# Transposing the B and C projections by DMA instead of on TensorE in a one-core hybrid SSD and attention layer

## The chip, the cores and the metric

The kernel runs on one core of a Trainium2 chip. The metric is the device time of one execution in microseconds (us), as the median of several runs. Engine names: PE is TensorE (PEld its weight loads), DVE is VectorE, ACT is ScalarE, POOL is GpSimd and SP is SyncE, which here issues the loads.

## The reference

One decoder layer on 256 tokens of width 2048, all in float32. What matters here is the state-space (SSD) group at its start:

```python
proj = rmsnorm(h) @ w_in                                  # z | x,B,C | dt | q | k | v
xbc = silu(causal_dwconv(xbc, conv_w, conv_b))            # 4 taps along the tokens, one filter a channel
xs, bm, cm = split(xbc)                                   # x: 2048 channels, B and C: 4 groups x 128 each
dt = softplus(dt_raw + dt_bias)
cb = einsum('bclgn,bcsgn->bgcls', Cc, Bc)                 # per group and chunk of 128 tokens
y_diag = einsum('bgecls,bcsgep->bclgep', cb * decay_in, X)
states = einsum('bclgn,bgecl,bclgep->bcgepn', Bc, decay_states, X)
```

After it come the gate z, a grouped norm, sliding-window attention, the output projection, a feed-forward part with a convolution of 3 taps, and a gated embedding.

## The kernel before

**Products.** Each product of 256 tokens goes in chunks of 512 columns. A weight slab (256 rows by 512 columns) is loaded on SP's queue (line 207, tile `w`, 7 slots), rounded to a short float on ACT (line 192, `wh`, 4 slots), its rest is taken on DVE (line 193, `wl`, 4 slots), and PE makes three products of each (lines 219 to 221, or 317 to 319 for B and C). So a slab of one chunk is 12 matmuls (2 row blocks, 2 token blocks, 3 products) and a chunk of the input projection is 8 slabs. A chunk's sums stand in a pair of PSUM tiles, `acc0` and `acc1`, one for each 128 tokens, in two buffers.

**Order.** B and C are computed together over all 16 row blocks while `xT` is loaded, and fill both pairs of `acc`; the products for dt come behind them (lines 337, 338). Then the code treats B, then C (lines 387 to 390), then the chain of dt (lines 392 to 435: transposed dt at line 394, softplus, running sums, a copy `scr` in DRAM), then group by group x, z, the scan and the gate (`ssd_x`, `ssd_gate`, `ssd_end`). The compiler's planner orders each engine's instructions by a simulated timeline, so they stand in its queue in another order than in the code; an engine then works strictly in the order of its queue and waits at its head.

**B and C.** `evac_scaled` (line 348) copies each half of the sums to SBUF on ACT (line 352, tiles `ct0`, `ct1`, one buffer, which C shares with B). `conv_chunk` (line 272) transposes it on PE, 4 channel blocks by 2 token blocks, so 8 transposes for B and 8 for C (line 279), into `tr`, a PSUM tile with two buffers. `conv_tile` (line 263) then makes the first tap on ACT (line 266) and three taps on DVE (line 268) out of PSUM into `BT` or `CT`. A SiLU on ACT follows (line 390). The `tr` tiles are taken in code order, so the one for dt (line 392) comes after the four of B and C. `BT` is read by the transpose at line 465 and with `CT` by the matmuls at line 456; `CT` again at line 499. x goes through the same `conv_chunk` (line 471).

**The feed-forward part** (lines 825 to 844) has the same convolution done in another way: ACT copies the sums to `u` (line 831), POOL takes the 32-bit numbers apart into two halves of 16 bits (line 833, `half`), SP issues a transposing DMA (line 835, `flip`), POOL puts the halves together (line 836, `uc`), and the convolution reads `uc` in SBUF (line 843).

Of the kernel before, what the change touches and what calls it, by code (L numbers as in the profile page):

```python
# [14 lines left out]
U16 = mybir.dt.uint16  # L15
# [5 lines left out]
P = 128  # L21
T = 256
NB = T // P
# [3 lines left out]
NC = 512  # L27
# [38 lines left out]
def hybrid_layer(  # L66
# [20 lines left out]
    nc = tc.nc  # L87
    V, S, G, PE = nc.vector, nc.scalar, nc.gpsimd, nc.tensor
# [13 lines left out]
    def nm(s):  # L102
        uid[0] += 1
        return f"{s}_{uid[0]}"
# [3 lines left out]
    def sb(pool, shape, tag, dt=F32, bufs=None):  # L108
        kw = {} if bufs is None else {"bufs": bufs}
        size = math.prod(shape[1:]) * (2 if dt in (mybir.dt.bfloat16, U16) else 4)  # L110
        tags = sizes.setdefault(pool.id, {})
        tags[tag] = max(tags.get(tag, 0), -(-size // 32) * 32 * (bufs or pool.bufs))
        return pool.tile(shape, dt, tag=tag, name=nm(tag), **kw)
# [7 lines left out]
    def acc_pair():  # L121
        return [ps_acc.tile([P, NC], F32, tag=f"acc{b}", name=nm(f"acc{b}")) for b in range(NB)]

    def tr_tile():
        return ps_tr.tile([P, NC], F32, tag="tr", name=nm("tr"))
# [14 lines left out]
    def load_first(k, pieces=1):  # L140

        xt = sb(xin, [P, T], "xt", bufs=6)
        nc.sync.dma_start(xt, xT[:, k, :])
        w = sb(wp, [P, KW, NC], "w", bufs=WR)
        n = KW // pieces
        for c in range(0, KW, n):
            cs = slice(c, c + n)
            nc.sync.dma_start(w[:, cs, :], w_in[cs, k // KW, :, (k % KW) * NC : (k % KW + 1) * NC].rearrange("c p n -> p c n"))
        return w, xt
# [26 lines left out]
    scw = sb(const, [P, 24 * 5], "scw")  # L176
# [86 lines left out]
    def conv_tile(ps, dst, taps, bias):  # L263

        n = len(taps)
        S.activation(out=dst, in_=ps, func=AF.Identity, scale=taps[n - 1], bias=bias)
        for s in range(1, n):
            V.scalar_tensor_tensor(  # L268
                out=dst[:, s:], in0=ps[:, : T - s], scalar=taps[n - 1 - s], in1=dst[:, s:], op0=ALU.mult, op1=ALU.add
            )  # L270

    def conv_chunk(src, dst, cw, ntap, c0):

        for half in range(2):
            tr = tr_tile().rearrange("p (a t) -> p a t", a=2)
            for i in range(2):
                f = half * 2 + i
                for b in range(NB):
                    PE.transpose(tr[:, i, b * P : (b + 1) * P], src[b][:, f * P : (f + 1) * P], ident)
            for i in range(2):  # L280
                f = half * 2 + i
                w = cw[:, (c0 + f) * (ntap + 1) : (c0 + f + 1) * (ntap + 1)]
                conv_tile(tr[:, i, :], dst[:, f, :], [w[:, j : j + 1] for j in range(ntap)], w[:, ntap : ntap + 1])
# [13 lines left out]
    acc_b, acc_c = acc_pair(), acc_pair()  # L297
    with xin_:
        wd = sb(xin, [P, KT, 32], "wd")
        dhl = sb(xin, [P, KT, 64], "dhl", F32R)  # L300
        for k in range(KT):
            w, xt = first[k] if k < len(first) else load_first(k)
# [23 lines left out]
            if k in (5, 9):  # L326
                b = k // 4 - 1
# [20 lines left out]
    def evac_scaled(acc, pool, tag, bufs=None):  # L348
        res = []
        for b in range(NB):  # L350
            t = sb(pool, [P, NC], f"{tag}{b}", bufs=bufs)
            S.activation(out=t, in_=acc[b], func=AF.Copy, scale=rx[:, b : b + 1])
            res.append(t)
        return res
# [29 lines left out]
    with tc.tile_pool(name="ssd", bufs=1) as sp, tc.tile_pool(name="dram", bufs=1, space=bass.MemoryType.DRAM) as dp:  # L384
        BT = sb(sp, [P, 4, T], "BT")
        CT = sb(sp, [P, 4, T], "CT")
        for c, (acc, dst) in enumerate(((acc_b, BT), (acc_c, CT))):
            t = evac_scaled(acc, sp, "ct", 1)
            conv_chunk(t, dst, scw, 4, 16 + 4 * c)
            S.activation(out=dst, in_=dst, func=AF.Silu)  # L390

        tr = tr_tile()
# [137 lines left out]
        with tc.tile_pool(name="rope", bufs=1) as rp:  # L530
# [3 lines left out]
            for j in range(HALF):  # L534
                f = float(np.float32(THETA) ** np.float32(-2.0 * j / ROPE))
# [332 lines left out]
    with tc.tile_pool(name="ple", bufs=2) as lp:  # L868
# [5 lines left out]
        for n in range(4):  # L874
            acc = acc_pair()
# [77 lines left out]
```

## Time and profile before

| | |
|---|---|
| median of 3 runs | 1437.21 us (1435.33 to 1437.77) |
| the profiled execution | 1435.81 us, of which its span from the first to the last instruction is 1434.1 us |
| busy share of the span | PE 99%, PEld 81%, DVE 69%, ACT 55%, POOL 20% |
| granted clock of PE | 0.999 of full speed |
| DMA | 292.62 MB, 204 GB/s on average |

Times in the rows are counted from the start of the span. The duration of a matmul overlaps the next one's, so what a matmul costs is read from the distance of two starts. An entry "[1.09 <-ACT ct L352]" says that the engine stood idle for 1.09 us before and that ACT's instruction of line 352 ended this. B and C are summed up until about 54 us, and the first reading of `CT` is at 105 us.

### The profile page before, as it was taken

The numbers are of one execution on the slowest core, as the hardware profiler recorded it, in microseconds if no ns is written. First come the engines' busy times: TensorE is split into PE (matmuls) and PEld (weight loads), VectorE is DVE, ScalarE is ACT, GpSimd is POOL, SyncE is SP. The second block draws the span as 40 slices with busy tenths as digits, with TensorE's granted clock in tenths as the row PEclk, the third lists the DMA queues.
The fourth block names the chain that finished last, engine by engine and source line by source line (L and its number), as shares of the span: only waits on it lengthen the run. The fifth ranks groups of instructions, "written<-read, shape, count | busy, mean of one in ns | idle before, by whom it ended". The sixth has DMA issues, their size and how long they took to land.

```text
span 1434.1 us, 18053 instructions
## 1 busy us (share of the span) xinstructions
PE 1421.9 (99%) x6516; PEld 1166.2 (81%) x6516; DVE 995.0 (69%) x1240; ACT 792.0 (55%) x1067; POOL 288.2 (20%) x234
## 2 busy tenths in 40 slices
PE   9999999999999999999999999999999999999998
PEld 6887888888877777888888888888888888888886
DVE  6678876766789889656667646765675577476854
ACT  6575555544576655556556446545554554455643
POOL 0002010008535422013143103201320131120000
PEclk9999999999999999999999999999999999999999
DMA  9666656556787777577787777867876876776671
GB/s 338 217 190 202 201 177 189 163 160 205 191 236 198 213 203 223 171 208 209 217 231 198 217 196 216 228 194 202 226 208 194 221 214 205 206 207 190 209 223 66
DMA packets 163466, 292.62 MB, mean 204 GB/s; under 512 B 93040, under 2 KB 95920, under 8 KB 162992
## 3 DMA queue, kind: packets, MB, share of 16 engines
q1 hardware_dynamic: 162944, 290.99, 69.8%
q8 instruction: 51, 0.84, 0.2%
q10 hardware_dynamic: 432, 0.48, 0.1%
q14 instruction: 39, 0.32, 0.1%
HBM read 268.32 MB, written 2.13 MB: 189 GB/s over the span
## 4 chain that ended last, share of the span: by engine, by line
PE 61%; DVE 1%; issue 0%; ACT 0%; DVEq 0%
PE acc L220 20%; PE acc L221 20%; PE acc L219 20%; PE tr L252 0%; DVE wl L193 0%; PE tr L731 0%; DVE h L359 0%; DVE den L713 0%; DVE sg L883 0%; ACT s L709 0%; DVE yl L193 0%; DVE s L698 0%; DVE nm L705 0%; DVE sg L884 0%; ACT sg L882 0%
## 5 line engine op out<-in xcount | busy, mean ns | idle before, releaser
L193 DVE TENSOR_TENSOR wl<-w,wh 128x1024 fp32r<-128x1024 f32 (+1 forms) x493 | 637.8, 1298 | 370.9 <-ACT wh L192 370.1
L192 ACT CAST wh<-w 128x1024 fp32r<-128x1024 f32 (+1 forms) x493 | 514.8, 1049 | 496.6 <-PE acc L221 446.5
L220 PE MATMUL acc<-wl,ah 128*128 128x512 f32 x1280 | 499.8, 390 | 1.2 <-DVE wl L193 1.2
L221 PE MATMUL acc<-wh,al 128*128 128x512 f32 x1280 | 499.7, 391 | 0.0
L219 PE MATMUL acc<-wh,ah 128*128 128x512 f32 x1280 | 498.6, 391 | 0.0
L220 PEld LDWEIGHTS acc<-wl,ah 128*128 128x128 f32 x1280 | 240.4, 188 | 51.6 <-DVE wl L193 1.6
L219 PEld LDWEIGHTS acc<-wh,ah 128*128 128x128 f32 x1280 | 240.4, 188 | 50.8 <-issue 1.2
L221 PEld LDWEIGHTS acc<-wh,al 128*128 128x128 f32 x1280 | 240.4, 188 | 50.1 <-issue 0.5
L221 PE MATMUL acc<-wh,gl 128*128 128x512 f32 x352 | 137.0, 389 | 0.0
L220 PE MATMUL acc<-wl,gh 128*128 128x512 f32 x352 | 137.0, 389 | 0.0
L219 PE MATMUL acc<-wh,gh 128*128 128x512 f32 x352 | 136.4, 389 | 0.0
L833 POOL COPY half<-u 128x1024 uint16<-128x1024 uint16 x44 | 60.7, 1393 | 263.1 <-ACT u L831 263.1
L219 PE MATMUL acc<-wh,yh 128*128 128x512 f32 x256 | 101.3, 396 | 0.8 <-DVE h L359 0.8
L220 PE MATMUL acc<-wl,yh 128*128 128x512 f32 x256 | 100.0, 391 | 0.6 <-DVE wl L193 0.6
L221 PE MATMUL acc<-wh,yl 128*128 128x512 f32 x256 | 99.6, 390 | 0.0
L836 POOL COPY uc<-flip 128x1024 uint16<-128x1024 uint16 x44 | 55.7, 1265 | 166.3 <-DMA flip<-half 166.3
L220 PEld LDWEIGHTS acc<-wl,gh 128*128 128x128 f32 x352 | 66.1, 188 | 13.7
L221 PEld LDWEIGHTS acc<-wh,gl 128*128 128x128 f32 x352 | 66.1, 188 | 13.7
L219 PEld LDWEIGHTS acc<-wh,gh 128*128 128x128 f32 x352 | 66.1, 188 | 13.6
L359 DVE TENSOR_TENSOR h<-h,acc 128x512 f32<-128x512 f32 x112 | 72.6, 677 | 1.1 <-PE acc L221 1.1
L268 DVE SCALAR_TENSOR_TENSOR cv<-uc,fcw,cv 128x254 f32<-128x254 f32 (+1 forms) x176 | 73.0, 475 | 0.0
L219 PEld LDWEIGHTS acc<-wh,yh 128*128 128x128 f32 x256 | 48.0, 188 | 14.4 <-issue 4.3
(229 smaller groups left out, 1129.5 us busy)
## 6 DMA issues: line engine op xcount, KB each, us to landing
w<-in_w_up_dram SPq DMA_DIRECT2D x176, 512.0 KB, 3.9
w<-in_w_in_dram SPq DMA_DIRECT2D x126, 512.0 KB, 4.1
w<-in_w_down_dram SPq DMA_DIRECT2D x88, 512.0 KB, 4.2
w<-in_w_out_dram SPq DMA_DIRECT2D x64, 512.0 KB, 4.2
w<-in_w_pg_dram SPq DMA_DIRECT2D x32, 512.0 KB, 4.3
seg<-scr SPq DMA_DIRECT2D x8, 512.0 KB, 5.4
xt<-in_xT_dram SPq DMA_DIRECT2D x16, 128.0 KB, 6.5
h<-in_x_dram SPq DMA_DIRECT2D x2, 1024.0 KB, 8.6
```

Of the source, the lines that this page charges most:

```text
L192: S.copy(hi, src)
L193: V.tensor_tensor(out=lo, in0=src, in1=hi.bitcast(F32), op=ALU.subtract)
L219: PE.matmul(acc[b], lhsT=hi, rhs=wh[:, i, :], start=(k == 0), stop=False)
L220: PE.matmul(acc[b], lhsT=hi, rhs=wl[:, i, :], start=False, stop=False)
L221: PE.matmul(acc[b], lhsT=lo, rhs=wh[:, i, :], start=False, stop=(k == total - 1))
L268: V.scalar_tensor_tensor(out=dst[:, s:], in0=ps[:, : T - s], scalar=taps[n - 1 - s], in1=dst[:, s:], op0=ALU.mult, op1=ALU.add)
L359: V.tensor_tensor(out=hs, in0=hs, in1=acc[b], op=ALU.add)
L833: G.tensor_copy(half.rearrange("p (a n) -> p a n", a=2), u_.bitcast(U16).rearrange("p (n a) -> p a n", a=2))
L836: G.tensor_copy(uc[:, :, b * P : (b + 1) * P].bitcast(U16).rearrange("p f (t a) -> p f t a", a=2), flip.rearrange("p (a f) t -> p f t a", ...
```

## The change

B and C are no longer transposed on PE. ACT evacuates B's sums to `ct` as before and C's to tiles of their own (`yc0`, `yc1`). For each half of 128 tokens, POOL takes the numbers apart into 16-bit halves, SP issues a transposing DMA and POOL puts the halves together in a tile `raw`; the convolution reads `raw` in SBUF. B uses the slots of tiles that come later (`z`, `Xd`, `xc`), C uses new ones (`xh`, `xf`, `xt`). The convolution's own instructions stay as they are, and x keeps its transposes on PE.

```diff
-        for c, (acc, dst) in enumerate(((acc_b, BT), (acc_c, CT))):
-            t = evac_scaled(acc, sp, "ct", 1)
-            conv_chunk(t, dst, scw, 4, 16 + 4 * c)
+        for c, (acc, dst, tags) in enumerate(((acc_b, BT, ("ct", "z", "Xd", "xc")), (acc_c, CT, ("yc", "xh", "xf", "xt")))):
+            t = evac_scaled(acc, sp, tags[0], 1 + c)
+            raw = sb(sp, [P, 4, T], tags[3])
+            for b in range(NB):
+                half = sb(sp, [P, 2 * NC], f"{tags[1]}{b}", U16)
+                G.tensor_copy(half.rearrange("p (a n) -> p a n", a=2), t[b].bitcast(U16).rearrange("p (n a) -> p a n", a=2))
+                flip = sb(sp, [P, 8, P], f"{tags[2]}{b}", U16)
+                nc.sync.dma_start_transpose(flip, half)
+                G.tensor_copy(
+                    raw[:, :, b * P : (b + 1) * P].bitcast(U16).rearrange("p f (t a) -> p f t a", a=2),
+                    flip.rearrange("p (a f) t -> p f t a", a=2),
+                )
+            for f in range(4):
+                i = 16 + 4 * c + f
+                w = scw[:, i * 5 : (i + 1) * 5]
+                conv_tile(raw[:, f, :], dst[:, f, :], [w[:, j : j + 1] for j in range(4)], w[:, 4:5])
             S.activation(out=dst, in_=dst, func=AF.Silu)
```

## Rows read from the trace of the kernel before

**Rows 1.** The page, busy time of an engine: us (share of the span) and instructions.
```profile
PE 1421.9 (99%) x6516; PEld 1166.2 (81%) x6516; DVE 995.0 (69%) x1240; ACT 792.0 (55%) x1067; POOL 288.2 (20%) x234
```

**Rows 2.** PE's waits over the whole span: us in total, times, longest us.
```profile
PE acc L220 <- DVE wl L193: 1.8, 2, 1.2
PE tr L279 <- ACT ct L352: 1.1, 1, 1.1
```

**Rows 3.** Timeline of PE, 56 to 125 us: start us, us, what.
```profile
56.74 0.41 PE L279 MATMUL tr<-ident,ct 128*128 128x128 f32 x2 [1.09 <-ACT ct L352]
56.90 0.48 PE L219 MATMUL acc<-wh,ah 128*128 128x512 f32 x1
...
60.17 0.39 PE L221 MATMUL acc<-wh,al 128*128 128x512 f32 x1
...
61.31 0.39 PE L220 MATMUL acc<-wl,ah 128*128 128x512 f32 x1
61.54 0.82 PE L279 MATMUL tr<-ident,ct 128*128 128x128 f32 x6
62.11 0.48 PE L219 MATMUL acc<-wh,ah 128*128 128x512 f32 x1
62.42 0.40 PE L220 MATMUL acc<-wl,ah 128*128 128x512 f32 x1
...
86.80 0.63 PE L394 MATMUL tr<-sel,hsq 64*128 64x32 f32 x4
...
104.99 0.60 PE L456 MATMUL ms<-CT,BT 128*128 128x128 f32 x4
...
124.21 0.50 PE L220 MATMUL acc<-wl,ah 128*128 128x512 f32 x1 [1.15 <-DVE wl L193]
```

**Rows 4.** Lines 833, 836 and 835: duration ns min/median/max, first and last start.
```profile
L833 POOL COPY half<-u x44: 1037/1043/2039, 630.5 to 1263.1; 128x1024 uint16<-128x1024 uint16 x44
L836 POOL COPY uc<-flip x44: 1155/1164/2112, 639.0 to 1273.5; 128x1024 uint16<-128x1024 uint16 x44
L835 SPq DMA_TRANSPOSE flip<-half x44: 1237/1239/1590, 634.4 to 1267.6; - x44
DMA to landing us min/median/max: 3.7/5.4/6.6
```

**Rows 5.** Timeline of ACT, one chunk of the feed-forward part: evacuation and convolution.
```profile
629.77 0.69 ACT L831 ACTIVATE u<-acc,rh 128x512 f32<-128x512 f32 x1 [0.37 <-PE acc L221]
...
645.63 2.08 ACT L266 ACTIVATE cv<-uc,fcw 128x256 f32<-128x256 f32 x4
```

**Rows 6.** Who waited for line 836 over the whole span: us, times.
```profile
  ACT cv L266: 4.7, 5
```

**Rows 7.** Timeline of POOL, 33 to 112 us: its first work after 33 us.
```profile
111.03 1.88 POOL L448 TENSOR_SCALAR_AFFINE_SELECT seg<-seg 128x1024 f32<-128x1024 f32 x1 [77.70 <-ACT wh L192]
```

**Rows 8.** Waits of SP's queue, 0 to 320 us: us in total, times, longest us.
```profile
SPq L207 <- DVE wl L193: 207.4, 84, 9.0
```

**Rows 9.** Groups of DVE, 45 to 110 us: busy us, mean ns, idle before.
```profile
L193 DVE TENSOR_TENSOR wl<-w,wh 128x1024 fp32r<-128x1024 f32 x20 | 24.4, 1221 | 12.1 <-ACT wh L192 11.7 <-issue 0.2
L268 DVE SCALAR_TENSOR_TENSOR BT<-tr,scw,BT 128x254 f32<-128x254 f32 x4 | 1.9, 475 | 0.0
```

**Rows 10.** The same groups, 630 to 1275 us, the feed-forward part.
```profile
L193 DVE TENSOR_TENSOR wl<-w,wh 128x1024 fp32r<-128x1024 f32 x238 | 312.4, 1315 | 235.9 <-ACT wh L192 235.9
L268 DVE SCALAR_TENSOR_TENSOR cv<-uc,fcw,cv 128x254 f32<-128x254 f32 x84 | 38.6, 475 | 0.0
```

**Rows 11.** Timeline of ACT, 62 to 65 us: the first tap of B and the next cast.
```profile
62.06 0.57 ACT L266 ACTIVATE BT<-tr,scw 128x256 f32<-128x256 f32 x1 [3.31 <-PE tr L279]
...
64.12 1.06 ACT L192 CAST wh<-w 128x1024 fp32r<-128x1024 f32 x1
```

**Rows 12.** Timeline of DVE, 62 to 86 us: taps of B and C.
```profile
62.66 2.81 DVE L268 SCALAR_TENSOR_TENSOR BT<-tr,scw,BT 128x255 f32<-128x255 f32 x6 [5.84 <-ACT BT L266]
...
85.55 0.47 DVE L268 SCALAR_TENSOR_TENSOR CT<-tr,scw,CT 128x253 f32<-128x253 f32 x1
```

## The prediction

> **What bounds the kernel now.** I read three views in turn. The busy table shows PE at work for 99% of the span and POOL for 20% [rows 1], so time is lost only where PE has more to do or stands still. PE's waits say how much of the second there is: 1.8 us in two waits for a weight's rest from DVE and 1.1 us in one wait for the evacuation of B are those of one microsecond or more behind the start-up [rows 2]. The timeline places them: the wait for B at 55.65 to 56.74 us, the longer wait for DVE just before 124.21 us [rows 3]. Between 56 and 320 us, where the SSD part ends, I found no other gap. So the stage that the change touches has 1.09 + 1.15 = 2.24 us of standing time and otherwise a PE that is full: an instruction taken off PE there shortens the kernel by what it takes in the row of starts, and everything on other engines costs nothing until a weight slab comes late.
>
> **The sum is made against** the profiled execution, 1435.81 us (span 1434.1). It lies 1.40 us under the median of the three runs, 1437.21, and within their spread; the sums below are put on the median. About 0.2% of it, 2.87 us, is what a measurement of this kernel can tell from no change.
>
> **Removed: 16 transposes on PE.** A usual matmul starts 0.228 us after the one before: from 60.17 to 61.31 us are five of them, 1.14 us [rows 3]. With six transposes between, the starts from 61.31 to 62.42 us are 1.11 us apart where two steps would be 0.456. So six cost 0.65 us, 0.109 each, and this includes the slow first matmul behind them. Sixteen cost 1.75 us. As a lower bound I take off the first two, which stand right behind the wait for B's evacuation [rows 3]: 14 x 0.109 = 1.5 us. The matmul behind them needs the same evacuation, for its sums go where B's stood; so the wait of 1.09 us stays, and I keep 1.75, because with the two gone that matmul can start at 56.74 instead of 56.90.
>
> **Added on POOL: eight copies.** Four that take apart, of 1.04 us, and four that put together, of 1.16 us [rows 4]: 8.8 us. POOL has nothing to do for 77.7 us up to 111.03 us [rows 7], so in itself this costs nothing; without that cover it would delay the masks of line 448.
>
> **Added on SP: four transposing DMAs,** 1.24 us of issue each [rows 4], 5.0 us, and each waits at the head of SP's queue for its half, with weight loads behind it. Those loads are early: up to 320 us SP waited 84 times, 207 us, because DVE had not yet freed a slot [rows 8]. Seven slots of 12 x 0.228 = 2.7 us each are 19 us of stock. Cost nothing; without the stock it would be up to 5 us.
>
> **The path of B and C gets longer.** Two half copies, one issue ahead of the second transpose, a landing and the last copy are 2 x 1.04 + 1.24 + 5.4 + 1.16 = 9.9 us [rows 4]; from 56.74, when the first evacuation was there, `raw` of B is complete at 66.6 us. At the pace of the feed-forward part, 645.63 - 629.77 = 15.9 us from evacuation to convolution [rows 5], it would be 56.74 - 0.69 + 15.9 = 71.9. Before, B's first tap was at 62.06 [rows 11]. C follows some 5 us of POOL behind B. `CT` is first read at 104.99 us [rows 3], and even 15 us more than the old end of C's taps at 86.0 [rows 12] meets that. Cost nothing, unless ACT waits for it at the head of its queue (below).
>
> **The convolution out of SBUF:** the taps on DVE are 475 ns from PSUM and 475 from SBUF [rows 9, 10]. Nothing.
>
> **POOL beside DVE.** With no work on POOL a split on DVE is 1221 ns [rows 9], in the feed-forward part, where POOL copies, 1315 [rows 10]. 238 x 0.094 = 22.4 us over 88 such copies (and ten products of POOL, which I leave in, so this is high) is 0.25 us of DVE a copy, 2.0 us for eight; the upper bound, if DVE stands for every copy in full, is 8.8. DVE was idle 5.84 us before B's first tap [rows 12], and that is when the half copies run. I take 2.0, hidden. [...]
>
> **What moves besides.** The transposed dt of line 394 ran at 86.80 us, just after C's last tap released a `tr` tile at 86.0 [rows 3, 12]. B and C no longer use those tiles, so the whole chain of dt can run some 30 us sooner, in the idle time of ACT and DVE near 60 us [rows 11, 12]. It is not what PE waits for, so I count it as nothing in the sum.
>
> **Sum:** -1.75 us and unchanged standing time: 1434.06 for the profiled execution, 1435.5 on the median, within 0.2%. Its own range is 1434.4 to 1437: 1.75 gone, up to 1.5 us of new or lost standing time, and about 1 us of spread.
>
> **First rival, faster.** The wait before 124.21 us was for a split that DVE made late, amid the decay tiles of the first group. If the dt chain goes early, those tiles go with it, and the wait can vanish: -1.75 - 1.15 = -2.9, 1434.3; if the planner also puts B's evacuation sooner and the wait of 1.09 goes, -4.0, 1433.2. For it speaks the freed `tr` tile, against it that the crowd may only move elsewhere. Chance 0.28, and I count it as faster though its first form lies on the boundary.
>
> **Second rival, slower: ACT waits for `raw` with casts behind it.** If the planner takes the path through the DMA for too short and leaves B's first tap near 62.06 us in ACT's queue, ACT stands there until 66.6 to 71.9, 4.5 to 9.8 us. Behind it is the cast of 64.12 [rows 11], for the fifth slab of x's first chunk (four slots hold the first four). That slab's split ended at about 64.12 + 1.06 + 1.22 = 66.4, and PE needs it at 56.74 + 4 x 2.74 = 67.7: 1.3 us of slack. PE then stands for 3.2 to 8.5 us, net +1.4 to +6.8, 1438.7 to 1444.0. It decides (over +2.87) once PE stands 4.6 us, which is `raw` of B complete after 68.0. Against it: in the feed-forward part the same chain is planned 15.9 us wide, ACT waited for POOL only 4.7 us in 5 of its convolutions [rows 6], and I found no gap of PE there. Chance 0.15.
>
> **Third rival, nothing left of the gain: DVE is held by POOL.** At the bound of 8.8 us less the 5.84 idle, splits are 3.0 us late, less 1.3 of slack is 1.7 us of standing PE: 1437.2. [...] The mean of 0.25 us a copy speaks against it. Chance 0.12.
>
> That the change does not do what it says is hardly open: the 16 transposes are gone from PE whatever the planner does.
>
> **The numbers.** Forecast 0.45, faster rival 0.28, slower rival 0.15, held DVE 0.12. Within 0.2% are the forecast and the third: 0.57. The predicted time is the forecast's, 1435.5. The range takes the lower end of the first rival with half a microsecond of spread, 1432.7, and the middle of the second, 1441.3.
>
> **What would show it.** Right: no line 279 for B and C on PE; eight POOL copies and four transposes at 57 to 75 us; PE's starts up to the end of the SSD part 1.5 to 2 us sooner; the wait of about 1.1 us at 55.65 still there, with ACT's evacuation as its end. First rival: line 394 near 60 us and no wait near 124. Second: ACT's line 266 of B idle for 4 us or more on POOL, and a PE wait on DVE's split near 68 us. Third: splits at 57 to 75 us of about 2 us. I am wrong if PE's total standing time in the SSD part changes by more than 1.5 us in either direction.

## The result and the profile after

The changed kernel takes 1442.04 us (median of 9 runs, 1440.18 to 1447.25) against 1437.23 us before (9 runs, 1435.33 to 1438.30): ratio 1.0043, 95% interval [1.0033, 1.0052]. It is slower by more than 0.2%, and above the range of 1432.7 to 1441.3 us. (The quotient of the two medians is 1.0033; the ratio on record is not formed from them.) The profiled execution took 1440.18 us, its span 1438.5; it is the fastest of the nine, so its rows show rather less of the loss than the median.

The busy table of the changed kernel answers [rows 1]: PE has 16 instructions less, POOL eight more, DVE is busy 11.8 us longer with the same number of instructions, most of it in the feed-forward part, through which PE runs as fast as before.

```profile
PE 1422.2 (99%) x6500; PEld 1163.9 (81%) x6500; DVE 1006.8 (70%) x1240; ACT 791.3 (55%) x1067; POOL 303.3 (21%) x242
```

PE's waits of the changed kernel over the whole span (us in total, times, longest us) answer [rows 2]. The wait for B's evacuation has become a shorter one of the dt transposition, but the waits for a split from DVE have grown from 1.8 to 6.6 us, 4.0 of them in one piece.

```profile
PE acc L220 <- DVE wl L193: 6.6, 3, 4.0
PE acc L219 <- DVE h L359: 1.3, 2, 1.1
PE tr L407 <- ACT hsq L341: 0.5, 1, 0.5
```

The timeline of PE in the changed kernel places them, beside [rows 3]. The dt transposition (now line 407) runs at 55.15 instead of 86.80 us. No wait is left near 124 us. The long one is at 87.18 to 91.17, where the kernel before had none.

```profile
55.15 0.63 PE L407 MATMUL tr<-sel,hsq 64*128 64x32 f32 x4 [0.46 <-ACT hsq L341]
...
86.57 0.61 PE L219 MATMUL acc<-wh,ah 128*128 128x512 f32 x2
91.17 0.79 PE L220 MATMUL acc<-wl,ah 128*128 128x512 f32 x1 [3.99 <-DVE wl L193]
91.76 0.63 PE L221 MATMUL acc<-wh,al 128*128 128x512 f32 x1
92.19 0.63 PE L220 MATMUL acc<-wl,ah 128*128 128x512 f32 x1
```

PE's busy time in stretches of the changed kernel (stretch, length, busy and instructions, granted clock, DMA share, GB/s) shows what followed: from 92 to 94 us the granted clock is 0.50 (it is so for all of the 2.84 us from 91.17 to 94.01), and matmuls start 0.43 us apart instead of 0.228. The same stretches of the kernel before are all at 1.00.

```profile
80.00:87.00 7.00, 7.00 (x32) 1.00 0.94 248
87.00:92.00 5.00, 1.01 (x3) 0.86 0.04 15
92.00:94.00 2.00, 2.00 (x6) 0.50 0.72 250
94.00:96.00 2.00, 2.00 (x10) 1.00 0.76 229
```

DVE's timeline in the changed kernel shows why the split at 89.91 was late. Nine taps of B in a row stood ahead of it, behind the first decay tiles (76.73 to 84.6 us), before which DVE was idle for 3.93 us. The last row, nine taps of C with POOL idle, took 3.73 us, where B's nine took 5.38. The first row, two small instructions of the dt chain, ran beside POOL's copies.

```profile
61.81 2.16 DVE L434 SCALAR_TENSOR_TENSOR adt<-dt,ea 128x32 f32<-128x32 f32 x2
...
76.73 0.17 DVE L458 TENSOR_TENSOR dec<-seg,acs 128x8 f32<-128x8 f32 x1 [3.93 <-DMA seg<-scr]
...
82.38 1.05 DVE L458 TENSOR_TENSOR dec<-seg,acs 128x8 f32<-128x8 f32 x1
83.47 1.22 DVE L460 TENSOR_TENSOR seg<-seg,acs 128x1024 f32<-128x1024 f32 x1
84.61 5.38 DVE L268 SCALAR_TENSOR_TENSOR BT<-xc,scw,BT 128x255 f32<-128x255 f32 x9
89.91 1.21 DVE L193 TENSOR_TENSOR wl<-w,wh 128x1024 fp32r<-128x1024 f32 x1
...
96.39 3.73 DVE L268 SCALAR_TENSOR_TENSOR CT<-xt,scw,CT 128x255 f32<-128x255 f32 x9 [0.69 <-ACT CT L266]
```

The same two instructions in the kernel before, with POOL idle (DVE's timeline):

```profile
96.32 0.29 DVE L421 SCALAR_TENSOR_TENSOR adt<-dt,ea 128x32 f32<-128x32 f32 x2
```

POOL's timeline of the changed kernel answers [rows 7]: its first new work is at 55.75, and `raw` of B (tile `xc`) is complete at 61.65 + 2.27 = 63.92 us. The second row, the last copy of C, took 1.63 us, where it takes 1.16 in e13; it ran beside B's taps, and so did the mask of line 461 behind it (85.67 us, 1.28 us).

```profile
61.65 2.27 POOL L395 COPY xc<-Xd 128x1024 uint16<-128x1024 uint16 x2 [1.91 <-DMA Xd<-z]
...
84.08 1.63 POOL L395 COPY xt<-xf 128x1024 uint16<-128x1024 uint16 x1 [0.66 <-DMA xf<-xh]
```

ACT's timeline of the changed kernel answers [rows 11]: B's first tap runs at 78.56, 14.6 us after its data were there, and 16.5 us later than before. ACT waited for nothing then; in its queue the tap stood behind the evacuation of x.

```profile
77.98 0.68 ACT L352 ACTIVATE ct<-acc,rx 128x512 f32<-128x512 f32 x1
78.56 2.07 ACT L266 ACTIVATE BT<-xc,scw 128x256 f32<-128x256 f32 x4
...
93.51 1.28 ACT L403 ACT_TABLE_LOAD   x1 [5.11 <-DVE BT L268]
```

**Where the time went.** I numbered PE's matmuls into `acc` from the start (every kernel here has 5904) and compared the start of the same number in two profiles. The table gives, for every profile, its start minus that in the profile of before, at five numbers that before reaches at the times in the head; behind 600 us all kernels run parallel. The runs e1 to e16 are told below. (Lines of the changed kernel are 13 higher from the convolution of C on than before's; in the runs they are another 7 to 9 higher where an order is written out.)

| profile | 57.2 | 80.1 | 95.3 | 325.0 | 600.2 | median us | 95% interval of the ratio |
|---|---|---|---|---|---|---|---|
| after | -1.14 | -1.95 | +1.89 | +0.60 | +4.36 | 1442.04 | 1.0033 to 1.0052 |
| e1 | -0.62 | +2.46 | +2.43 | +3.73 | +5.42 | 1441.84 | 1.0027 to 1.0053 |
| e2 | -0.44 | -1.27 | +2.49 | +1.20 | +3.34 | 1439.58 | 1.0016 to 1.0036 |
| e3 | -0.13 | -0.60 | -0.32 | -2.71 | +0.10 | 1435.64 | 0.9986 to 1.0005 |
| e4 | -1.00 | -2.58 | -4.36 | +3.88 | +11.88 | 1447.71 | 1.0074 to 1.0099 |
| e5 | -0.56 | -0.56 | -0.56 | -0.22 | +2.00 | 1437.32 | 0.9989 to 1.0007 |
| e6 | -2.07 | -3.64 | -3.03 | -0.39 | +3.47 | 1439.83 | 1.0009 to 1.0027 |
| e7 | +0.38 | +1.17 | +1.23 | -1.03 | -0.91 | 1435.97 | 0.9980 to 0.9997 |
| e8 (before) | -0.19 | -0.19 | -0.19 | +1.37 | +1.50 | 1437.30 | one run |
| e9 | -0.24 | -1.08 | -2.86 | +2.89 | +8.53 | 1444.08 | 1.0043 to 1.0069 |
| e10 | -0.42 | -0.38 | -0.38 | +0.26 | +2.19 | 1437.50 | 0.9999 to 1.0016 |
| e11 | -1.74 | -1.70 | -1.69 | -1.00 | +1.45 | 1436.74 | 0.9993 to 1.0010 |
| e12 | -0.48 | -1.31 | -2.60 | +4.05 | +5.81 | 1441.78 | 1.0025 to 1.0051 |
| e13 | -0.43 | -1.27 | -2.49 | -3.78 | +2.24 | 1437.04 | 0.9989 to 1.0007 |
| e14 | -0.37 | -1.21 | -2.44 | -3.73 | -2.23 | 1433.61 | 0.9973 to 0.9990 |
| e15 (e11) | -0.55 | -0.51 | -0.51 | -1.07 | +1.41 | 1437.14 | one run |
| e16 (before) | -0.59 | -0.55 | -0.55 | -0.74 | -0.13 | 1435.68 | one run |

For the changed kernel: 0.81 us are gained from 57 to 80 us. In that stretch the kernel before has six of B's transposes and all eight of C's, which stand here:

```profile
75.59 0.60 PE L279 MATMUL tr<-ident,ct 128*128 128x128 f32 x4
76.72 0.60 PE L279 MATMUL tr<-ident,ct 128*128 128x128 f32 x4
```

By the same count the six are worth 0.67 us (57.2 to 65 us) and the eight 0.92 (75 to 80.1), and the four matmuls of dt's running sums, which now come at 64.3 us instead of 99.3, take 0.78 back. From 80 to 95 us 3.84 are lost: 3.99 of standing and some 1.4 of matmuls at half clock (half of the 2.84), less 0.8 for dt's transposition, which now comes ahead of 57 us, and some 0.9 for transposes of `BT` and x that PE does only later here. Then 1.29 are gained: the wait of 1.15 before 124 us and dt's running sums, less those later transposes. From 325 to 600 us, in the attention part, which the edit does not touch, 3.76 are lost. e8 and e16, the kernel before again, show how far a single profile scatters: up to 1.6 us in the SSD part, 0.6 in attention. Two kernels whose order in attention is the same can lie further apart there (e3 and e7 below).

### The profile page after: what moved, and what is told of

Its sections match the earlier page's. It is cut to its first block, busy times and chain, and to the rows that moved or that the text cites. A ratio compares the mean times of both kernels' runs of the same rounds, so it can differ in the third digit from the quotient of the medians.

```text
span 1438.5 us, 18028 instructions
## 1 busy us (share of the span) xinstructions
PE 1422.2 (99%) x6500; PEld 1163.9 (81%) x6500; DVE 1006.8 (70%) x1240; ACT 791.3 (55%) x1067; POOL 303.3 (21%) x242
## 3 DMA queue, kind: packets, MB, share of 16 engines
HBM read 268.32 MB, written 2.13 MB: 188 GB/s over the span
## 4 chain that ended last, share of the span: by engine, by line
PE 61%; DVE 1%; issue 0%; ACT 0%; DVEq 0%
PE acc L220 20%; PE acc L221 20%; PE acc L219 20%; PE tr L252 0%; DVE wl L193 0%; PE tr L744 0%; DVE h L359 0%; DVE den L726 0%; ACT s L722 0%; DVE sg L896 0%; DVE yl L193 0%; DVE s L711 0%; DVE nm L718 0%; DVE sg L897 0%; ACT sg L895 0%
## 5 line engine op out<-in xcount | busy, mean ns | idle before, releaser
L193 DVE TENSOR_TENSOR wl<-w,wh 128x1024 fp32r<-128x1024 f32 (+1 forms) x493 | 645.2, 1313 | 365.2 <-ACT wh L192 364.4
```

The costliest lines, as they stand in the source:

```text
L193: V.tensor_tensor(out=lo, in0=src, in1=hi.bitcast(F32), op=ALU.subtract)
```

## The experiments

### The order of before: e1, e2

The compiler's planner had put PE, ACT and DVE into another order in the SSD part, and ACT, DVE, POOL and SP in the attention part too. In e1 the changed kernel is held in before's order on PE, ACT and DVE throughout. The order is written out by lists (`ORDER`) and held by `NoSync` edges:

```diff
+    for eng, runs in ORDER.items():
...
+        for one, two in zip(seq, seq[1:]):
+            tc.add_manual_dep(two, one.name, mybir.DependencyInfo(mybir.DependencyClass.NoSync, mybir.DependencyReason.DATA), reason="order")
```

> The changed kernel with the instructions of PE, ACT and DVE held in the order of the kernel before (16 transposes taken out of PE's), POOL and SP left to the planner. Theory (the loss is the planner's new order, in the SSD part and in attention): only the price of the parts is left, -1.75 us for the transposes and at most 2 us of new wait, because raw of B was complete at 63.9 us and B's first tap stands at 62.06 in this order: 1435.5 to 1437.5 beside 1437.2, no gap of 3 us on PE. Rival (the work added on POOL and SP, and POOL in DVE's way, cost the time): about as slow as the changed kernel, 1440 to 1443.

It took 1441.84 us, as long as the changed kernel, so the theory fell; but it lost its time elsewhere: 3.08 us from 57 to 80 us, and 1.69 in attention. In ACT's timeline of e1 the first tap now waits at the head of the queue, with evacuations and casts behind it:

```profile
64.72 0.60 ACT L273 ACTIVATE BT<-xc,scw 128x256 f32<-128x256 f32 x1 [6.40 <-POOL xc L402]
```

On PE of e1 that ends in a wait for a split, and again in a stretch at half clock (timeline, then stretches with the columns as above):

```profile
70.82 0.79 PE L227 MATMUL acc<-wl,ah 128*128 128x512 f32 x1 [2.13 <-DVE wl L200]
```

```profile
69.00:71.00 2.00, 0.18 (x1) 0.89 0.00 0
71.00:73.00 2.00, 2.00 (x5) 0.50 0.64 70
```

So the old order does not fit the longer path, as the prediction's second rival has it; the new order does not make this mistake, but the opposite one.

e2 holds only the attention part (ACT, DVE, POOL, SP) in before's order, with the same edges (between `hT = Lhs(...)` and `rh = finish_rstd(...)`); the SSD part is the changed kernel's.

> The changed kernel with the attention part's instructions on DVE, ACT, POOL and SP held in the order of the kernel before; the SSD part as in the changed kernel. Theory (3.7 us of the loss arise in attention, from its order alone): PE passes from 325 to 547 us of the kernel before in its old time within 0.7 us, total about 1438.3. Rival (attention is slower for another reason, as start-up scatter or the shifted arrival): total stays at 1441 to 1443.

1439.58 us: 2.46 less than the changed kernel, though over the 1438.3 expected, and attention's profile is 2.14 us over before's, where 0.7 were expected. The gap near 87 us stays (3.62 us). Two fifths (by the ratios) to half of the loss is thus the attention part's order.

### The parts of the change: e3, e4, e5, e7

e3 has neither the transposes nor what takes their place (so B and C go untransposed into the convolution, and what is computed of them is another thing); the planner is free.

```diff
-            raw = sb(sp, [P, 4, T], tags[3])
-            for b in range(NB):
...
-                conv_tile(raw[:, f, :], dst[:, f, :], [w[:, j : j + 1] for j in range(4)], w[:, 4:5])
+                conv_tile(t[f // 2][:, f % 2 * T : (f % 2 + 1) * T], dst[:, f, :], [w[:, j : j + 1] for j in range(4)], w[:, 4:5])
```

> B and C are convolved without being transposed at all: eight POOL copies and four transposing DMAs are left out, so the output is another. The planner is free. Theory (order): B's taps come early again, the gap of 4 us near 87 us is gone or under 1.5 us, and the attention part's order is again another one, so the total lies anywhere within 4 us of 1435.5. Rival (POOL, SP and their contention cost the time): 1435.5 within 1 us, with attention as fast as before.

The SSD part gains 2.58 us from 57 to 325 us; the fourteen transposes there (1.6), the wait before 124 us (1.15) and dt's transposition, now ahead of 57 us (0.8), less a new wait of 0.56, make 3.0. Attention gives 2.81 back in the profile, and the median is that of before. No POOL copy and no DMA is there to cost anything. But e7 below has the very same order of POOL, DVE, ACT and SP in attention and takes 0.12 us there, so order alone does not make these 2.81 either.

e5 is the reverse: the kernel before in its own order, with all eight POOL copies and the four transposing DMAs beside it, which nothing reads.

```diff
+            raw = sb(sp, [P, 4, T], tags[3])
+            for b in range(NB):
...
+            conv_chunk(t, dst, scw, 4, 16 + 4 * c)
```

> The kernel before, with its 16 transposes on PE and with PE, ACT and DVE held in its own order, and beside it all that the change adds on POOL and SP: the eight copies and four transposing DMAs of B and C run, and nothing reads what they make. Theory (the path costs time only because something waits for it in the queue): within 1.5 us of the kernel before, 1435 to 1438, no new gap of PE over 1 us. Rival (POOL in DVE's way, and transposes among the loads on SP, cost the time by themselves): 1439 or more.

1437.32 us, ratio 0.9998: the copies and transposing DMAs cost nothing that can be measured.

e4 is the changed kernel with the first work of DVE on dt held behind C's last tap, as it stood before:

```diff
-        for b in range(NB):
-            V.scalar_tensor_tensor(
+        with tc.issue_after(last.ins):
+            for b in range(NB):
+                V.scalar_tensor_tensor(
```

> The changed kernel with the chain of dt on DVE held behind C's last tap, as it stood before through the tr tiles. Theory (the first group's decay tiles, early because of dt, crowd DVE together with B's late taps): the gap near 87 us falls under 1.5 us. Rival (B's late taps alone make the weight split late): a gap of 2.5 us or more stays between 75 and 100 us. The attention part may again have another order; total 1436 to 1441.

The worst of all, 1447.71, where 1436 to 1441 were expected. B's taps are no earlier than in the changed kernel (ACT's timeline of e4):

```profile
79.56 2.08 ACT L266 ACTIVATE BT<-xc,scw 128x256 f32<-128x256 f32 x4
```

Yet PE is 4.36 us ahead at 95 us and the wait near 87 is gone, as the theory had it: late taps alone need not make the split late; without the early decay tiles, and in the order that the planner then chose, they did not. By 325 us 8.2 us are lost, most of it in four waits at 127 to 161 us of up to 1.85 us each: for a split, twice for the scan's `yc` and once for `yh`; attention, in yet another order, loses 8.0 more. Holding dt back is no cure.

e7 leaves everything of the kernel before and only takes dt's transposition out of the `tr` tiles:

```diff
-        tr = tr_tile()
+        tr = ms_tile()
```

> The kernel before with one word changed: the tile for the transposed dt comes from another PSUM pool (ms), so the chain of dt runs early as in the changed kernel; B and C stay on PE, nothing is added. The planner is free. Theory (time comes and goes with the planner's order in parts that the edit does not touch): the wait before 124 us goes or moves, and attention's order is another one and its time differs by over 0.7 us from before; total anywhere from 1433 to 1441. Rival (order matters only where the edit is): attention as before within 0.5 us, total 1434.5 to 1436.5.

1435.97 us, ratio 0.9989. The early dt chain alone, without any DMA, is worth 1.6 us by the ratio (0.4 to 2.9 by its interval), and 1.41 us from 57 to 325 us in its profile, of which 0.8 is only dt's transposition moved ahead of 57 us. The planner, free here, gave attention another order than before's, and its profile takes 0.12 us more there: e7's rival was right that such an order need not cost time.

### A hand order and a control: e6, e8

e6 is e1 with some thirty instructions moved by hand in the lists, so that B's taps stand where their data arrive, and with B's two transposing DMAs side by side on SP.

> The changed kernel with PE, ACT and DVE in the order of the kernel before, as in e1, but for some 30 places written by hand: B's sums are evacuated ahead of the cast that stood before them, C's right behind, the casts and splits of the next three weight slabs stand ahead of B's first tap, PE takes x's first chunk slab by slab, and B's two transposes stand side by side on SP. Theory (e1 lost its time because casts and splits stood behind a tap that waited for raw): the 1.75 us and most of the 1.1 us wait at 55 us are gained, no gap of PE between 57 and 100 us over 0.7 us, 1433 to 1435 beside 1436.2. Rival (the path costs in itself): 1438 or more.

PE gained 1.57 us from 57 to 80 us, which is the fourteen transposes, and then lost it: in before's order DVE makes two later splits too late, as it does in e8, where the same two waits took 0.99 and 1.38 us. PE's timeline of e6:

```profile
119.21 0.50 PE L228 MATMUL acc<-wl,ah 128*128 128x512 f32 x1 [1.36 <-DVE wl L201]
...
123.87 0.50 PE L228 MATMUL acc<-wl,ah 128*128 128x512 f32 x1 [1.38 <-DVE wl L201]
```

With attention's 3.9 us in its profile it came to 1439.83, where 1433 to 1435 were expected. It points to the old crowd of decay tiles at 110 to 124 us, which only an early dt clears.

e8 is the kernel before in its own order, run to see the scatter.

> The kernel before once more, with the same order on every engine, for a second profile of it: how far PE's progress through the parts scatters by itself. Expected: start-up within 1 us, the part from 325 to 547 us within 1 us, no gap of PE over 1.5 us behind the start-up.

### The late split alone: e9, e12

e9 holds the changed kernel in its own order on all engines and moves only four splits of DVE. In words of its queue, with slabs counted from x's first chunk:

```diff
-9 taps of B, split of slab 12, 2 taps, split of slab 13, 1 tap, splits of slabs 14 and 15
+split 12, 2 taps of B, split 13, 3 taps, split 14, 3 taps, split 15, 4 taps
```

> The changed kernel held in its own order on every engine, with one thing moved: on DVE the four weight splits (L193) that stood behind and among the last twelve of B's taps are spread through those twelve, the first of them ahead of all. Theory (the main loss is DVE's: nine taps of 0.60 us stood ahead of the split that PE waited for at 87.18): the gap of 3.99 us goes, and with it the stretch at granted clock 0.50 after it (some 1.5 us); PE stands 4 to 5 us earlier at 95 us than in the changed kernel's profile, and the run ends 2 to 4.5 us below 1442.0, at 1437.5 to 1440, since the attention's order is still the changed one and keeps its loss. Rival (the slack is spent elsewhere): the gap only moves to the next split, or B's and C's later taps hold the first group's SSD back, and the time stays at 1441 to 1443. Rival (the reordered attention is what counts): the gap goes, but attention gives it back, 1440.5 to 1442.

The gap at 87 us went as expected, and the time rose to 1444.08. PE came to 93.79 without a wait and then stood longer than before, now for B itself, whose SiLU could only follow the last tap. PE's timeline of e9:

```profile
93.79 0.39 PE L229 MATMUL acc<-wl,ah 128*128 128x512 f32 x1
99.09 0.47 PE L487 MATMUL tr<-ident,BT 128*128 128x128 f32 x1 [4.92 <-ACT BT L412]
```

So the place of the split was not the cause. With B's taps begun as late as in the changed kernel, something must wait: the split if the taps go first, B's transposition if the split does. My main theory for e9 fell; its first rival had the mechanism, at too small a price.

e12 is the same move with attention in before's order, and e10's four DMAs.

> The changed kernel with e9's move of the four weight splits, the attention part in the order of the kernel before, and the four unread DMAs of e10. If the split behind the taps, attention's order and the shift are all that the change lost by, what is left is what it was meant to bring: 16 transposes (1.75 us) and the wait before 124 us (1.2 us) less than before, so 1434 to 1435.5. If only the first two count, 1435.5 to 1437. If something else in the SSD part holds (the wait for the decays, POOL beside DVE), 1437 to 1440, with its gap before 325 us.

1441.78, over all that was expected (1434 to 1440), with the same stand (4.91 us at 99.36): nothing else could show while B was late.

### Shifted semaphores: e10, e11, e15, e16

In the trace of before the 605 DMAs that are issued signal eight semaphores in turn, 75 or 76 times each, and in the changed kernel's 609 do; four more DMAs shift the turn of all later ones by four. e10 is e5 with four more small DMAs, so that the turn is the old one again; e11 is the kernel before in its own order with these four alone.

```diff
+        for k in range(4):
+            nc.sync.dma_start(dp.tile([P, 64], F32, tag=f"spare{k}", name=f"spare{k}"), acs)
```

> The kernel before in its own order on PE, ACT and DVE, with the POOL copies and the four DMA transposes of the change unused beside it (as in e5), and four more DMAs of 32 KB on SP that nothing reads, so that eight are added and every later DMA signals the same one of the eight completion semaphores as in the kernel before. In e5's profile the attention part, which the edit doesn't touch and whose order was that of before, took 2.2 us more than in before's. Theory (the shift by four semaphores changes what waits for what later on): attention comes back to within 0.5 us of before's, with gaps at 547 and 557 us only, and the run ends at 1436 to 1437. Rival (the shift is without effect, attention's loss in the profiles is scatter or comes with the place of POOL's copies in time): gaps near 406 and 460 us stay, attention +1.5 to +2.5, and the time stays at 1437 to 1438.

> The kernel before in its own order, with nothing added but four DMAs of 32 KB on SP that nothing reads: every later DMA signals a semaphore four further on than in before. Theory (shift): attention takes 1.5 to 2.5 us more than in before's profile, with gaps near 406 and 460 us; time 1438 to 1439.5. Rival: attention within 0.5 us of before's, time 1436.5 to 1438, as the kernel before itself.

In attention e10 lost 1.93 and e11 2.45 us against before's profile: the loss is there with the turn restored as with it shifted, so the shifted semaphores are not its cause. In the medians it hardly shows (1436.74 for e11, 1436.26 for before beside it). e15 is e11's kernel run once more, e16 before's.

> e11's kernel once more (the kernel before in its own order, four unread DMAs of 32 KB added), one profile. If e11's attention part (2.45 us longer than before's) is a lasting cost of the four DMAs, it is 1.5 us or more again; if it is scatter between executions of one program, it may fall to 0 to 1 us.

> The kernel before once more, one profile. If attention's time scatters between executions by some 2 us whatever the kernel, one of the profiles of before (two so far at 0.0 and 0.1 us) can show 1 us or more; if the added DMAs are what costs, it is within 0.3 us a third time.

e15 lost 2.48 in attention again, e16 only 0.61, e8 0.13. So with added DMAs, and with PE, ACT and DVE in before's order in attention, the profiles are 1.5 to 3.9 us longer there (e1, e2, e5, e6, e10, e11, e12, e14, e15). POOL and SP run in before's order there too in all nine, as their traces show, so order is no part of this loss. Nor is it sure that the DMAs are: e3 and e7 differ by 2.7 us there with one order and no DMA added. The cause, and why the medians of e5 and e11 don't show it, stay open.

### B's taps when their data are there: e13, e14

e13 holds the changed kernel in its own order and moves only B's taps: four on ACT, twelve on DVE.

```diff
 ACT:
 cast of slab 8
+4 first taps of B
 casts of slabs 9 and 10, exp of dec, cast of slab 11, evacuation of x
-4 first taps of B
 DVE:
 split of slab 8
+3 taps of B
 split of slab 9
+9 taps of B
 first decay tiles, with the splits of slabs 10 and 11 between them
-9 taps of B, split of slab 12, 2 taps, split of slab 13, 1 tap, splits of slabs 14 and 15
+splits of slabs 12 to 15
```

> The changed kernel held in its own order on every engine, with B's taps alone moved: the four on ACT (2.07 us) from 78.56 to right behind the cast at 67.77, the twelve on DVE (0.42 to 0.60 us each) from 84.61 to the idle 70 to 76.7 us; B's SiLU and all else stay in their places. Theory (B's taps were scheduled 14.6 us after their data were there, and crowded DVE when they came): no wait over 0.5 us between 57 and 115 us, no stretch at granted clock 0.50, PE at 95 us 3.5 to 5.5 us earlier than in the changed kernel's profile and at 325 us 2 to 4 us earlier; time 1437.5 to 1439.5. Rival (the SSD part is bound by C, whose second transpose is issued at 73.56 and which lands at 83.4): PE stands for C near 105 us instead, PE at 325 us within 1 us of the changed kernel's, time 1441 to 1443.

1437.04 us, 5.0 less than the changed kernel (0.9998 against 1.0043 of before). From DVE's timeline of e13: the taps now stand where DVE was idle for 3.93 us, and the four splits run in a row.

```profile
70.69 1.27 DVE L277 SCALAR_TENSOR_TENSOR BT<-xc,scw,BT 128x255 f32<-128x255 f32 x3
72.47 1.23 DVE L202 TENSOR_TENSOR wl<-w,wh 128x1024 fp32r<-128x1024 f32 x1 [0.52 <-ACT wh L201]
73.61 4.54 DVE L277 SCALAR_TENSOR_TENSOR BT<-xc,scw,BT 128x255 f32<-128x255 f32 x9
...
86.86 5.51 DVE L202 TENSOR_TENSOR wl<-w,wh 128x1024 fp32r<-128x1024 f32 x4
```

On PE of e13 the largest wait from 57 to 325 us is this one, and the granted clock is 1.00 in every stretch from 57 to 112 us (timeline, then stretches):

```profile
88.12 0.50 PE L229 MATMUL acc<-wl,ah 128*128 128x512 f32 x1 [0.25 <-DVE wl L202]
```

```profile
87.00:92.00 5.00, 4.75 (x21) 1.00 0.52 147
92.00:96.00 4.00, 4.00 (x22) 1.00 0.88 316
```

PE gains 3.35 us from 57 to 325 us against before, as much as the fourteen transposes, the wait before 124 us and the moved dt transposition make (1.6 + 1.15 + 0.8 - 0.25). At 325 us it is 4.38 us ahead of the changed kernel, where 2 to 4 were expected, and the time is 0.5 us under the range. So the late start of B's taps, on a DVE that the early decay tiles had filled, is the cause of the SSD part's loss, and the rival, C's second half landing late, fell. What remains in e13 is attention, +6.02 in its profile, in the same order as the changed kernel's +3.76. PE's waits there, 325 to 600 us of e13:

```profile
PE acc L228 <- DVE h L368: 4.0, 4, 2.2
PE acc L229 <- DVE wl L202: 0.7, 1, 0.7
PE sc L716 <- POOL qT L667: 0.5, 1, 0.5
```

e14 adds to that move before's order in attention, so it is e2 with B's taps early.

> The same move of B's taps in e2 (the changed kernel with the attention part in the order of before). e2 took 1439.6 with a gap of 3.63 us at 87.86. Theory: the gap goes and 1435 to 1437 is left, PE at 325 us 1.5 to 3 us earlier than in before's profile. Rival (C, or the attention part in any order, gives it back): 1438 to 1440.

1433.61 us, ratio 0.9981 [0.9973, 0.9990]: faster than both kernels, and 1.4 us below the range expected. PE's waits in the same stretch of e14:

```profile
PE sc L716 <- DVE s L720: 1.2, 1, 1.2
PE acc L229 <- DVE wl L202: 1.1, 2, 0.7
PE acc L228 <- DVE h L368: 0.7, 1, 0.7
```

The longest wait of e13 there is at 454 to 456 us, and the rows ahead of it are these, of DVE, of POOL and of PE, and PE's stretch behind it:

```profile
452.29 2.07 DVE L733 TENSOR_TENSOR es<-nm,rows 128x4 f32<-128x4 f32 x1
454.29 1.21 DVE L202 TENSOR_TENSOR wl<-w,wh 128x1024 fp32r<-128x1024 f32 x1
```

```profile
452.20 2.14 POOL L667 COPY s<-flip 128x2048 uint16<-128x2048 uint16 x1 [0.82 <-DMA flip<-half]
```

```profile
456.24 0.47 PE L228 MATMUL acc<-wh,ah 128*128 128x512 f32 x1 [2.17 <-DVE h L368]
```

```profile
456.00:459.00 3.00, 2.76 (x8) 0.69 0.59 180
```

The same instruction of e14, ahead of POOL's copy, which starts at 448.31 there:

```profile
448.22 0.16 DVE L733 TENSOR_TENSOR es<-nm,rows 128x4 f32<-128x4 f32 x1
```

POOL's timeline of e14:

```profile
448.31 3.22 POOL L667 COPY s<-flip 128x2048 uint16<-128x2048 uint16 x1 [0.98 <-DMA flip<-half]
```

A DVE instruction on 128 x 4 numbers took as long as the POOL copy beside it, and the split and the sum that PE waited for stood behind it. Around this place DVE and POOL have the same instructions in the same order in both kernels: in e14 DVE's came 0.09 us before the copy, in e13 0.09 us behind it. So in these two profiles it is not the order at this place that decides but which of two engines comes first by a tenth of a microsecond, and this may be why one order takes such different times in attention. That the order as a whole costs time is shown by two pairs of kernels that differ in it alone (3.4 us from e13 to e14, 2.5 from the changed kernel to e2), not where each microsecond goes.

## Why the prediction was wrong

The loss is the sum of three terms, each with the change of one thing between two kernels: B's taps late, 1442.04 - 1437.04 = 5.0 us; attention in the changed order, 1437.04 - 1433.61 = 3.4; and the change itself, 1433.61 - 1437.23 = -3.6. By the ratios they are 6.5, 2.4 and -2.7. (The median of before was 1436.19 to 1437.28 in the five sets of runs, so about one microsecond of each may be scatter.) Taken the other way, over e2 instead of e13, the ratios give the same 6.5 and 2.4.

**Step by step.** *The 16 transposes, 1.75 us:* right. Fourteen gave 0.67 + 0.92 = 1.6 us from 57 to 80 us. *POOL's copies and SP's transposing DMAs, nothing:* right, by e5, though the issues took 1.35 to 3.08 us and not 1.24. *The wait at 55.65 stays at 1.09:* wrong by 0.6, dt's transposes now stand there and wait 0.46. *The wait before 124 us stays:* wrong, it vanished as the first rival said; e7, with nothing but an early dt, gives 0.9989. *POOL beside DVE, 2.0 us and hidden:* too small, and perhaps not hidden (third rival below). PE's standing time in the SSD part went from 2.24 to 0.46 + 3.99 = 4.45 us, more than the 1.5 us of change that the prediction named as the sign of being wrong.

**The step that failed** is "The path of B and C gets longer", and its "Cost nothing". `raw` of B was there at 63.92, sooner than the 66.6 worked out, so the length was not the fault. I compared it with the first reading of `CT` at 104.99, as if the path were ready when its data are, and asked only whether ACT might stand at its head. I did not ask where the planner would put B's taps. It put them 14.6 us after the data, behind the evacuation of x, on a DVE full of decay tiles and splits. B's own reader, the transposition of `BT` (line 465 before, 487 in e9), is nearer than `CT`'s: it runs at 90.45 us in the kernel before, and e9 shows PE reaching it at 94.17. C's `raw` was complete at 84.08 + 1.63 = 85.71, 21.8 us behind B's and not some 5, which by e13 cost nothing.

**The second step that failed** is "What moves besides", with "so I count it as nothing in the sum". The early dt chain, which I foresaw, brings the decay tiles to 76.7 us, which is what B's late taps met on DVE; with dt held, in e4, the wait near 87 us is gone. And the prediction took the edit's reach to end with the SSD part. The planner also reordered the attention part, and that cost about as much as the whole change brings (2.4 and 2.7 us by the ratios).

**The rivals.** The first had the mechanism and the sum: 1433.2 to 1434.3 worked out, 1433.61 in e14 (1434.5 by its ratio), when order does not spoil it. The second had the sign and half a mechanism: its wait of ACT for `raw` does not occur in the changed kernel, whose planner errs the other way, but it is what e1 shows (6.40 us on ACT, where 4.5 to 9.8 were worked out; 1441.84 us, within its 1438.7 to 1444.0). That the time fits is partly luck: PE stood 0.51 + 2.13 us there, less than the 3.2 to 8.5 worked out, and the half clock and attention made up the rest. The third, DVE held by POOL, shows in the rows: 5.38 - 3.73 = 1.65 us on B's nine taps and 2.16 - 0.29 = 1.87 on the two dt instructions are already more than the 2.0 counted for eight copies. The taps stood right ahead of the late split, so up to 1.65 of its 3.99 us may come from there, part of it from POOL's mask. Its sign, splits of about 2 us at 57 to 75 us, did not come: they took 1.21 to 1.23. In e13 a 128 x 4 instruction that took 0.16 us in e14 took 2.07 beside a copy of 2.14: 1.91 us more, nearly the copy in full, as this rival's bound counts it. The mean of 0.25 us a copy, which I took against it, is one of the feed-forward part and says nothing of the places where the held instruction stands ahead of a split.

Not settled: why the planner placed the taps so late, the 2.5 us that attention's profiles show with four unread DMAs, and how much of attention's loss is order and how much the chance of which engine comes first.

## What to carry to other kernels

An operation that leaves the bound engine is worth its time only if the order made for the rest still feeds that engine; where a planner orders the program, ask of each moved producer when it will be *queued*, not only when its data are there, and compare the order of parts that the edit does not touch. When a wait appears, don't move the late instruction forward before asking what is late behind it: e9 turned 3.99 us of standing into 4.92. Holding both kernels in written-out orders, and then moving one thing, told apart in two runs what freely planned variants could not.

## What the runs showed of the hardware

After PE had stood 3.99 us its granted clock in the changed kernel was 0.50 for 2.84 us with PE fully busy; it was 0.50 too after 2.13 us in e1, and 0.69 on average over 3 us after 2.17 us in e13. Not every stand did this: after 1.83 us at 462 us in the changed kernel, and after 1.09 and 1.15 us in the kernel before, it stayed at 1.00. So a stand can cost more than its length: by my estimate some 1.4 us more in the changed kernel, half of the 2.84. Small DVE instructions beside a POOL copy can take as long as the copy: 2.07 us instead of 0.16 in e13, beside a copy of 2.14, and 2.16 instead of 0.29 for two in the changed kernel, beside two copies of 2.27 together. ACT stood at the head of its queue with later work ready: 5.11 us up to 93.51 in the changed kernel, for B's taps on DVE, while `raw` of C, which its first taps behind B's SiLU read, was complete at 85.71. The four transposing DMAs out of and into SBUF landed 4.2 to 10.5 us after their issue, where those of the feed-forward part took 3.7 to 6.6 [rows 4]; the last, issued at 73.56 us, was the slowest, and from 80 to 87 us the DMA engines had a share of 0.94. And a kernel with nothing added but four unread DMAs of 32 KB showed 2.45 and 2.48 us more in a part 250 us later, in two profiles, without a change of the median; that the DMAs are the cause is not shown.
